# Second MLP product by Strassen's method in a phase of its own, and a mask matmul padded from 42 to 128 rows, in a two-layer trunk on one core

## Chip, cores and metric

One Trainium2 chip, one core. The metric is the device time of one execution in microseconds (us), the median of several runs.

## The reference, cut to what matters

Two layers of a diffusion trunk work on 1024 latent and 256 context tokens of width 1024, all in fp32. Each layer is a normalised input projection, four groups of heads (state-space "SSD", attention, linear recurrence, differential attention), an output projection, and an MLP with a gated residual. The context tokens are updated in layer 0 alone. What the change touches:

```python
def sq_relu_mlp(u, w1, w2):
    return jnp.square(jax.nn.relu(u @ w1)) @ w2
...
    v_l = modulate(rms_norm(h_lat, p['norm2_g']), mod_l[3], mod_l[4])
    h_lat = h_lat + mod_l[5] * sq_relu_mlp(v_l, p['w_mlp1'], p['w_mlp2'])
```

`w1` is 1024 x 4096, `w2` is 4096 x 1024.

## The kernel before

**Products.** Data lie with features on the 128 partitions and tokens along the free axis. Each fp32 operand is split into a rounded high part and the rest (`uh`, `ul`; `wh`, `wl`; `hh`, `hl`), and a product is three matmuls: high x high, high x low, low x high. The second part of a name tells the operand that lies in the array as weights, the first the one that streams.

**Order.** The class `Sched` records operations (`op`, `tt`, `stt`, `act`, `mms`, `copy`, `dma`), and `run` then writes the program: a list scheduler with planned costs (`due` gives each operation its latest start from the sum of PE costs before it) picks the operation for each engine, subject to quotas of buffers of each stream (`s.cls("S", ...)`: 30 tiles of 1288 columns; `w`, `raw`, `h`: smaller ones). An operation that may run on two engines (`copy("ANY", ...)`) goes to the one that is free first by the plan. On the chip each engine runs its own instructions in the order so fixed, and waits on semaphores. All instructions come from `_emit` (L606), so that one line stands for all of them and the profile is read by tile names. All DMAs are issued from one queue, SP.

**The MLP** (`mlp`, L1565). The normalised input `v` stands in 8 tiles (`uh`, `ul`). `m1(f)` computes 128 of the 4096 hidden features: `w_cols` loads 128 columns of `w_mlp1` (`wr`, split into `wh`, `wl`), `gemm_fm` makes 24 matmuls for each group of tokens (512, 512 and in layer 0 another 256 of context), then relu (`r`), square, and the split into `hh`, `hl`. `m2` takes two such `f`, loads two blocks of 128 rows of `w_mlp2`, and for each group of tokens and each of 8 feature tiles makes 6 matmuls in one PSUM bank, which DVE adds, times the gate `mod`, into the residual tile `hR` (self.hT), kept in SBUF. `m1` and `m2` alternate, so that nothing of the hidden layer is kept. In layer 0 the context group stands last in each `m2`. After the MLP of layer 0 comes the norm of layer 1 (squares `sq`, sums `sts`, mean `lnm`, then `lx` and `uh`, `ul`), after that of layer 1 the store: transposes `cst,hR` by PE, copies `oo`, DMAs to `out`.

**The fill** (`layer`, `fill_rate`). In layer 0 the matmuls of layer 1's modulation (`wm,cT`) are mixed into the recorded stream of operations at a rate that is set there.

**The mask matmul** (`ssd_group`). 36 times in a run a matmul of one column of `pick`, broadcast to 128 columns, with `acr`, 42 rows of cumulated decays, spreads one row over all partitions; ACT reads the bank (`wk`).

Of the kernel before, what the change touches and what calls it, by code (L numbers as in the profile page):

```python
# [10 lines left out]
F32 = mybir.dt.float32  # L11
F32R = mybir.dt.float32r
AF = mybir.ActivationFunctionType
ALU = mybir.AluOpType
# [141 lines left out]
class Sched:  # L156
# [131 lines left out]

# [1 line left out]
    def act_cost(self, out, in_, func, **kw):  # L290
# [87 lines left out]

# [1 line left out]
    def due(self):  # L380
# [226 lines left out]
NT, NL = 1280, 1024  # L607
CO, CW = 1028, 1284
GROUPS = ((0, 512), (512, 512), (1024, 256))
EPS = 1e-6  # L610
SW, WW = 1288, 1056
# [36 lines left out]
class Trunk:  # L648
# [4 lines left out]
    def __init__(self, tc, nc, A, out, pools, dbg=None):  # L653
        self.A, self.out, self.dbg = A, out, dbg or {}
        s = self.s = Sched(tc, nc)
        sb, ps = pools
        self.sb = sb
        s.cls("S", sb, 30, SW, dict(u=16, ssd=8, lru=11, sw=2, qk=4, qv=2, ssdr=1, gk=4, dk=4, gv=2, dv=1, gq=2, dq=1, mo=2, gP=4, dP=8, gT=5, dT=5, mix=16, hT=8, hid=7, x=7, wm=10, st=5))
        s.cls("w", sb, 6, WW)
        s.cls("raw", sb, 3, WW)  # L660
        s.cls("h", sb, 4, 512, dict(ln=2, lq=3, mlp=4, go=1, do=1, asq=1, ssd=3, mod=1, out=3, load=2))
        s.cls("m", sb, 8, 48, dict(ln=3, att=2, qk=4, ssd=2))
        s.psum(ps, dict(mm=(0, 1, 2, 3), m4=(0, 1, 2, 3, 4, 5), ln=(4, 5, 3), att=(3, 0), tr=(6, 7), pv=(6,), ax=(6,),
                        ssd=(4, 5), lru=(6, 7), mod=(7,), ev=(6,), qk=(3,), st=(6, 7)))
        self.nconst = 0
        self.L = [dict(), dict()]
        self.fill, self.fill_rate, self.fill_at = None, 0, 0.0
# [6 lines left out]

# [1 line left out]
    def setup(self):  # L676
        s, A = self.s, self.A
        self.cst = self.const(448, "cst")
        s.dma(self.cst.v, A["cst"])
        c = self.cst  # L680
        self.ident, self.mf, self.mb = c[:, 0:128], c[:, 128:256], c[:, 256:384]
        self.blk2, self.inv_ln, self.inv128 = c[:, 384:386], c[:, 386:387], c[:, 387:388]
        self.nhalf, self.tiny, self.ones32 = c[:, 388:404], c[:, 404:405], c[:, 406:438]
        self.pick = self.const(10, "pick", dt=F32R)[0:42, :]
        s.copy("DVE", self.pick, c[0:42, 438:448])
        self.cT = self.const(8 * 32, "cT")
        self.consts_a(0)
        x = s.tile("h", 512, F32, "load", "cx")
# [187 lines left out]

# [1 line left out]
    def split_w(self, raw, n):  # L878
# [59 lines left out]

# [1 line left out]
    def load_x(self, gi):  # L940
# [106 lines left out]

# [1 line left out]
    def conv(self, out, raw, wcols, bcol, W=CW):  # L1049
# [28 lines left out]

# [1 line left out]
    def lru_weights(self, l):  # L1080
# [73 lines left out]

# [1 line left out]
    def ssd_dt(self, l, dtraw):  # L1156
        s, L = self.s, self.L[l]
        c = self.ssdc
        dt, dta, w1, w2, w3 = (c[:, 80 * i:80 * i + 80] for i in range(5))
        nac, dec, te = w3, w2, w1  # L1160
        x = dtraw
# [4 lines left out]
        pb = s.tile("psum", 512, F32, "ssd", "pac")  # L1166
# [10 lines left out]
        R = s.tile("S", SW, F32R, "ssdr", "acr")  # L1177
        s.op("POOL", [("memset", dict(ap=R[0:42, 0:1024].f, constant=0.0))], 1300)
        n4 = nac.r("p (t d g h) -> p g d h t", t=10, d=2, g=2)
        for g in range(2):  # L1180
            pb = s.tile("psum", 512, F32, "ssd", "par")
            s.transposes([dict(out=pb[0:10, 128 * i:128 * i + 128], in_=n4[:, g, i // 2, i % 2], identity=self.ident)
                          for i in range(4)])
            hi, lo = R[0:10, 512 * g:512 * g + 512], R[32:42, 512 * g:512 * g + 512]
# [5 lines left out]
    def ssd_group(self, l, g, xs, B, C, zmake):  # L1190
        s, L = self.s, self.L[l]
# [3 lines left out]
        for src, dst, eng in ((B, Bt, "ANY"), (xs, xt, "ANY")):  # L1195
            for b0 in (0, 4, 8):
                n = min(4, 10 - b0)
# [30 lines left out]
        for i, c in enumerate(order):  # L1228
# [5 lines left out]
            pb = s.tile("psum", 512, F32, "ssd", "pbc")  # L1234
            s.mms([dict(out=pb.v, lhsT=self.pick[:, c:c + 1].bc([42, 128]), rhs=self.acr[0:42, 512 * g:512 * g + 512],
                        start=True, stop=True)])
# [58 lines left out]

# [1 line left out]
    def qk_post(self, l, bank, off, H, d, gain, t, dst, rq=None):  # L1297
# [75 lines left out]

# [1 line left out]
    def att_open(self, l, kind, idx):  # L1375
# [153 lines left out]

# [1 line left out]
    def out_proj(self, l, gis, ks):  # L1531
# [19 lines left out]
        for f in range(8):  # L1551
# [7 lines left out]
            for gi in gis:  # L1559
# [3 lines left out]
                s.stt(h, bank[:, 0:gn], self.modcol(l, 2, 0 if g0 < NL else 1, f), h, ALU.mult, ALU.add)  # L1563

    def mlp(self, l, v, gis):  # L1565
        s, A = self.s, self.A
        hid = {}

        def m1(f):
            w = self.w_cols(A["w_mlp1"][l], 128 * f)  # L1570
            hh = s.tile("S", SW, F32R, "hid", "hh")
            hl = s.tile("S", SW, F32R, "hid", "hl")
            for gi in gis:
                g0, gn = GROUPS[gi]
                bank = self.gemm_fm(w, v, g0, gn)
                r = s.tile("h", 512, F32, "mlp", "r2")
                s.relu(r[:, 0:gn], bank[:, 0:gn])
                s.tt(r[:, 0:gn], r[:, 0:gn], r[:, 0:gn], ALU.mult)
                s.copy("ANY", hh[:, g0:g0 + gn], r[:, 0:gn])
                s.tt(hl[:, g0:g0 + gn], r[:, 0:gn], hh[:, g0:g0 + gn].f, ALU.subtract)  # L1580
            hid[f] = (hh, hl)

        def m2(fs):
            ws = [self.w_rows(A["w_mlp2"][l], 128 * f) for f in fs]
            for gi in gis:
                g0, gn = GROUPS[gi]
                for ft in range(8):
                    bank = s.tile("psum", 512, F32, "m4", "pm2")
                    o = bank[:, 0:gn]
                    calls = []  # L1590
                    for f, (wh, wl) in zip(fs, ws):
                        xh, xl = hid[f][0][:, g0:g0 + gn], hid[f][1][:, g0:g0 + gn]
                        h, lo = wh[:, 128 * ft:128 * ft + 128], wl[:, 128 * ft:128 * ft + 128]
                        calls += [dict(out=o, lhsT=h, rhs=xh), dict(out=o, lhsT=h, rhs=xl), dict(out=o, lhsT=lo, rhs=xh)]
                    for i, c in enumerate(calls):
                        c.update(start=(i == 0), stop=(i == len(calls) - 1))
                    s.mms(calls)
                    h = self.hT[ft][:, g0:g0 + gn]
                    s.stt(h, o, self.modcol(l, 5, 0 if g0 < NL else 1, ft), h, ALU.mult, ALU.add)

        m1(0)
        m1(1)
        for p in range(16):
            if p < 15:
                m1(2 * p + 2)
            m2((2 * p, 2 * p + 1))
            if p < 15:
                m1(2 * p + 3)

# [18 lines left out]
    def layer(self, l):  # L1628
# [84 lines left out]
        if l == 0:  # L1713
            self.consts_a(1, self.norm_end)
            self.consts_b(1, self.norm_end)
            self.fill, self.fill_rate = itertools.chain(*[self.mod_round(1, r) for r in range(3)]), 0.5
        self.mlp(l, v, gis)
# [56 lines left out]
```

## Time and profile before

| what | us |
|---|---|
| median of 3 runs (3348.85 to 3358.43) | 3353.89 |
| span of the profiled execution (no time outside it is given) | 3352.2 |
| PE busy | 3258.6 |
| DVE busy | 2171.1 |
| ACT busy | 1166.4 |
| POOL busy | 147.1 |

A page's busy time counts an engine as busy from the start of an instruction to its modelled end, so a PE that is never idle is not a PE that could not be used better. The MLP of layer 0 runs from about 911 to 1846 us, that of layer 1 from about 2625 to 3342 us. A timeline gives the start and the duration of every instruction; the step between two starts is what a stream of them costs.

### The profile page before, as it was taken

What the parts mean: (1) busy time and instruction counts of PE and PEld (TensorE: products, weight loads), DVE (VectorE), ACT (ScalarE), POOL (GpSimd) and SP (SyncE); (2) the same over time, 40 slices, a digit from 0 to 9 for tenths busy, and PEclk for the clock granted to TensorE, in tenths of its full rate; (3) what the DMA queues carried; (4) which work ended last, traced back from release to release, by engine and by line L of the source; (5) the groups of instructions that cost most, each with busy time, mean ns of one, the idle gap of its engine ahead of it and who ended that gap; (6) DMA issues with size and microseconds to landing.
All of it is one profiled execution on the core that took longest, in us unless ns stands there. A gap on an engine that the chain in (4) does not pass through costs nothing. (4 is left out here: it accounts for less than half of the span.)

```text
span 3352.2 us, 45841 instructions
## 1 busy us (share of the span) xinstructions
PE 3258.6 (97%) x18456; PEld 2622.8 (78%) x18456; DVE 2171.1 (65%) x3785; ACT 1166.4 (35%) x2026; POOL 147.1 (4%) x168
## 2 busy tenths in 40 slices
PE   8999989999999999999999999999999999999999
PEld 6877786677688888887887888886677788888887
DVE  4787789894565555554556688689883655555554
ACT  5554447772311110101112554438771311111111
POOL 0010040000000000000000010030000000000000
PEclk9999999999999999999999989989999999999999
DMA  8443261416212222212110321151433111111111
GB/s 247 140 125 97 89 175 41 110 35 232 70 48 75 72 79 67 78 57 85 42 45 26 118 73 50 57 154 39 97 116 121 41 51 51 51 44 46 49 50 57
DMA packets 253868, 276.51 MB, mean 82 GB/s; under 512 B 22876, under 2 KB 212184, under 8 KB 253656
## 3 DMA queue, kind: packets, MB, share of 16 engines
q1 hardware_dynamic: 253656, 273.59, 27.0%
q8 instruction: 145, 2.38, 0.3%
q14 instruction: 67, 0.55, 0.1%
HBM read 218.75 MB, written 54.79 MB: 82 GB/s over the span
## 5 line engine op out<-in xcount | busy, mean ns | idle before, releaser
L606 DVE SCALAR_TENSOR_TENSOR hR<-banks,mod,hR 128x512 f32<-128x512 f32 x720 | 497.2, 697 | 420.4 <-PE banks L606 420.4
L606 PE MATMUL banks<-uh,wh 128*128 128x512 f32 (+1 forms) x1808 | 682.4, 377 | 5.8 <-ACT cvr L606 1.9
L606 PE MATMUL banks<-uh,wl 128*128 128x512 f32 (+1 forms) x1808 | 669.1, 370 | 1.7 <-DVE wl L606 1.7
L606 PE MATMUL banks<-ul,wh 128*128 128x512 f32 (+1 forms) x1808 | 669.0, 370 | 1.3 <-DVE ul L606 1.2
L606 ACT ACTIVATE wh<-wr 128x1024 fp32r<-128x1024 f32 (+2 forms) x193 | 189.5, 992 | 1050.7 <-PE banks L606 1009.9
L606 PE MATMUL banks<-hh,wh 128*128 128x512 f32 (+1 forms) x1280 | 476.7, 372 | 0.0
L606 PE MATMUL banks<-hl,wh 128*128 128x512 f32 (+1 forms) x1280 | 475.5, 371 | 0.0
L606 PE MATMUL banks<-hh,wl 128*128 128x512 f32 (+1 forms) x1280 | 474.8, 371 | 0.0
L606 PEld LDWEIGHTS banks<-uh,wh 128*128 128x128 f32 x1808 | 341.3, 189 | 98.8 <-issue 26.1
L606 PEld LDWEIGHTS banks<-uh,wl 128*128 128x128 f32 x1808 | 340.6, 188 | 65.4 <-DVE wl L606 3.0
L606 PEld LDWEIGHTS banks<-ul,wh 128*128 128x128 f32 x1808 | 341.1, 189 | 61.5 <-DVE ul L606 3.7
L606 DVE TENSOR_SCALAR_CACHE_REDUCE P<-banks,rq 128x1280 f32<-128x1280 f32 (+1 forms) x216 | 301.3, 1427 | 29.4 <-PE banks L606 28.1
L606 DVE TENSOR_TENSOR r<-r 128x512 f32<-128x512 f32 x160 | 102.2, 639 | 333.6 <-ACT r L606 331.4
L606 PEld LDWEIGHTS banks<-hh,wh 128*128 128x128 f32 x1280 | 240.8, 188 | 53.5 <-DVE hR L606 5.3
L606 ACT ACTIVATE P<-P,am 128x1280 f32<-128x1280 f32 (+1 forms) x216 | 273.4, 1272 | 21.1 <-DVE P L606 19.8
L606 PEld LDWEIGHTS banks<-hh,wl 128*128 128x128 f32 x1280 | 240.4, 188 | 44.7
L606 PEld LDWEIGHTS banks<-hl,wh 128*128 128x128 f32 x1280 | 240.6, 188 | 43.3
L606 PE MATMUL banks<-wh,uh 128*128 128x256 f32 (+2 forms) x784 | 250.4, 319 | 6.0 <-DVE qkw L606 4.2
L606 DVE TENSOR_TENSOR wl<-wr,wh 128x1024 fp32r<-128x1024 f32 (+2 forms) x204 | 230.4, 1137 | 27.6 <-ACT wh L606 26.1
L606 PE MATMUL banks<-ks,qt 128*128 128x512 f32 (+1 forms) x800 | 220.8, 387 | 20.2 <-DVE P L606 15.7
L606 PE MATMUL banks<-wl,uh 128*128 128x256 f32 (+2 forms) x784 | 226.3, 289 | 0.0
L606 PE MATMUL banks<-wh,ul 128*128 128x256 f32 (+2 forms) x784 | 225.5, 288 | 0.0
(241 smaller groups left out, 4341.0 us busy)
## 6 DMA issues: line engine op xcount, KB each, us to landing
wr<-in_w_mlp_dram SPq DMA_DIRECT2D x128, 512.0 KB
wm<-in_w_mod_dram SPq DMA_DIRECT2D x96, 512.0 KB
wr<-in_w_in_dram SPq DMA_DIRECT2D x40, 512.0 KB
ks<-dk SPq DMA_DIRECT2D x64, 160.0 KB
qt<-dq SPq DMA_DIRECT2D x72, 128.0 KB
wr<-in_w_out_dram SPq DMA_DIRECT2D x64, 128.0 KB
hd<-hT SPq DMA_DIRECT2D x8, 640.0 KB
ks<-gk SPq DMA_DIRECT2D x16, 320.0 KB
```

The costliest lines, as they stand in the source:

```text
L606: getattr(e, method)(**args)
```

## The change

The MLP becomes two phases. `mlp` first writes the residual to DRAM (`he`), which frees its 8 tiles. `mlp_up` computes, for 16 pairs of feature tiles, relu and square on 1024 tokens, takes the pair and the two halves of the tokens as a 2 x 2 block matrix, forms the sums T1 to T4 on DVE, and writes seven operands of 128 x 512 to DRAM (`hp`); the context's hidden features go there already split (`hc`). `mlp_down` then works in four quarters of four pairs. For each of seven products (A11, A12, S3, A22, S2, S1, S4; in layer 0 also A21 for the context) it forms the sum of the `w_mlp2` blocks in place (`wr`), splits it (`wa`), loads the operand (`hs`, three buffers), splits it (`kb`), makes for each of 4 column blocks 12 matmuls in a bank, and adds the bank into 14 accumulator tiles (`ka`). In the last quarter it loads the residual again (`hR`) and combines the accumulators into it. Beside this, `pick` and `acr` get 128 rows in place of 42 (the added rows of the mask are zero), and the fill rate goes from 0.5 to 0.9.

```diff
-        s.cls("S", ..., mix=16, hT=8, hid=7, x=7, wm=10, st=5))
+        s.cls("S", ..., mix=16, hT=8, hid=10, ka=14, kb=7, kr=5, kc=4, x=7, wm=10, st=5))
-        s.cls("h", sb, 4, 512, dict(ln=2, lq=3, mlp=4, go=1, ...))
+        s.cls("h", sb, 4, 512, dict(ln=2, lq=3, mlp=4, hs=3, go=1, ...))
-        self.pick = self.const(10, "pick", dt=F32R)[0:42, :]
-        s.copy("DVE", self.pick, c[0:42, 438:448])
+        self.pick = self.const(10, "pick", dt=F32R)
+        s.copy("DVE", self.pick.v, c[:, 438:448])
-        s.op("POOL", [("memset", dict(ap=R[0:42, 0:1024].f, constant=0.0))], 1300)
+        s.op("POOL", [("memset", dict(ap=R[:, 0:1024].f, constant=0.0))], 1300)
-            s.mms([dict(out=pb.v, lhsT=self.pick[:, c:c + 1].bc([42, 128]), rhs=self.acr[0:42, 512 * g:512 * g + 512],
+            s.mms([dict(out=pb.v, lhsT=self.pick[:, c:c + 1].bc([128, 128]), rhs=self.acr[:, 512 * g:512 * g + 512],
...
+    def mlp_up(self, l, v, gis):
...
+            for e in range(2):
+                w = self.w_cols(A["w_mlp1"][l], 128 * (2 * p + e))
+                r = s.tile("S", SW, F32, "hid", "hr")
...
+                    bank = self.gemm_fm(w, v, g0, gn)
+                    o = r[:, g0:g0 + gn]
+                    s.relu(o, bank[:, 0:gn])
+                    self.square(o, o)
...
+            s.tt(T1, b12, b11, ALU.subtract)
+            s.tt(T2, b22, T1, ALU.subtract)
+            s.tt(T3, b22, b12, ALU.subtract)
+            s.tt(T4, b21, T2, ALU.subtract)
+            for i, z in ((0, b11), (1, b21), (2, T3), (3, T4), (4, T2), (5, T1), (6, b22)):
+                s.dma(d[:, 512 * i:512 * i + 512], z)
...
+    def mlp_down(self, l, gis):
...
+        def halves(piece):
+            t = s.tile("w", WW, F32R, "", "wa")
+            hi, lo = t[:, 0:512], t[:, 512:1024]
+            s.copy("ANY", hi, piece)
+            s.tt(lo, piece, hi.f, ALU.subtract)
...
+        def operand(p, i):
+            h = s.tile("h", 512, F32, "hs", "hs")
+            s.dma(h.v, self.hp[p][:, 512 * i:512 * i + 512])
+            t = s.tile("S", SW, F32R, "kb", "kb")
...
+        for q in range(4):
...
+            for i, name in enumerate(("A11", "A12", "A21", "S3", "A22", "S2", "S1", "S4")):
...
+                        bank = product(ws, xs, m, 512)
+                        a = at(pi, m)
+                        if q == 0:
+                            s.copy("ANY", a, bank.v)
+                        else:
+                            s.tt(a, bank.v, a, ALU.add)
...
+                    if name == "S1":
+                        s.tt(at(5, m), at(5, m), at(4, m), ALU.add)
+                        s.tt(at(2, m), at(2, m), at(5, m), ALU.add)
+                        add(h, m + 4, 0, 512, 512, at(2, m))
+                    if name == "S4":
+                        s.tt(at(6, m), at(6, m), at(5, m), ALU.add)
+                        add(h, m, 0, 512, 512, at(6, m))
...
     def mlp(self, l, v, gis):
...
+        for k in range(8):
+            s.dma(self.hd2[k][:, 0:n], self.hT[k][:, 0:n], after=self.norm_end)
+        self.hT = None
+        self.mlp_up(l, v, gis)
+        self.flush()
+        self.mlp_down(l, gis)
...
-            self.fill, self.fill_rate = itertools.chain(*[self.mod_round(1, r) for r in range(3)]), 0.5
+            self.fill, self.fill_rate = itertools.chain(*[self.mod_round(1, r) for r in range(3)]), 0.9
```

In counts, the program has 16,410 matmul instructions where it had 16,794, and 1,337 DMA issues where it had 825.

The passage from layer 0 to layer 1 on PE, before (`hh`, `hl` with 256 columns: context part of the last `m2`; `uh`, `ul`: input projection of layer 1):

```order
L606 MATMUL banks<-hl_14026,wh_14244 128x256
L606 MATMUL banks<-hh_14024,wl_14258 128x256
L606 MATMUL banks<-hh_14301,wh_14260 128x256
L606 MATMUL banks<-hl_14303,wh_14260 128x256
L606 MATMUL banks<-hh_14301,wl_14268 128x256
L606 MATMUL banks<-uh_6411_14494,wh_14377 128x512
L606 MATMUL banks<-ul_6412_14498,wh_14377 128x512
```

The same place on PE in the changed kernel (`kb`, `wa`: last product of the latent tokens; `sq`, `sts`, `lnm`: sums, mean and broadcast of the norm):

```order
L606 MATMUL banks<-kb_15043,wa_15037 128x512 x3
L606 MATMUL banks<-sq_15137,cst_66 32x512
L606 MATMUL banks<-sq_15146,cst_66 32x512
L606 MATMUL banks<-cst_66,sts_15157 128x1 x4
L606 MATMUL banks<-cst_66,lnm_15174 128x128 x4
L606 MATMUL banks<-sq_15160,cst_66 32x512
L606 MATMUL banks<-sq_15172,cst_66 32x512
L606 MATMUL banks<-sq_15195,cst_66 32x512
L606 MATMUL banks<-sq_15202,cst_66 32x512
L606 MATMUL banks<-uh_7263_15198,wh_15050 128x512
```

The product that stood between the latent tokens' last update and the new layer is gone from there; only the norm's own small matmuls are left. On DVE the changed kernel has at this place, from the last addition of a bank (`ka<-banks`) to the first low part of the new operand (`ul`):

```order
L606 TENSOR_TENSOR ka_5991_12566<-banks,ka_5991_12566 128x512
L606 TENSOR_TENSOR ka_5991_12566<-ka_5991_12566,ka_5947_12476 128x512
L606 SCALAR_TENSOR_TENSOR hR_7026_14807<-ka_5991_12566,mod_47_142,hR_7026_14807 128x512
L606 TENSOR_TENSOR ka_5745_12036<-ka_5745_12036,ka_5937_12444 128x512
L606 TENSOR_SCALAR lnm_15174<-banks 128x4
L606 TENSOR_TENSOR ka_5745_12036<-ka_5745_12036,ka_5937_12444 128x512
L606 SCALAR_TENSOR_TENSOR hR_7027_14821<-ka_5745_12036,mod_47_142,hR_7027_14821 128x512
L606 SCALAR_TENSOR_TENSOR hR_7028_14832<-ka_5745_12036,mod_47_142,hR_7028_14832 128x512
L606 TENSOR_TENSOR ka_5750_12053<-ka_5750_12053,ka_5947_12476 128x512
L606 SCALAR_TENSOR_TENSOR lx_15190<-hR_7023_14703,gs_4643_9448,banks 128x512
L606 SCALAR_TENSOR_TENSOR lx_15193<-hR_7024_14713,gs_4643_9448,banks 128x512
L606 TENSOR_TENSOR ka_5750_12053<-ka_5750_12053,ka_5947_12476 128x512
```

Sums of accumulators, updates of the residual and the norm's `lx` share the engine here; one more update and the `ul` follow. The end of the program on DVE, before (each row takes a bank of the last `m2` into the residual):

```order
L606 SCALAR_TENSOR_TENSOR hR_9516_20568<-banks,mod_4791_10044,hR_9516_20568 128x512
L606 SCALAR_TENSOR_TENSOR hR_9517_20585<-banks,mod_4791_10044,hR_9517_20585 128x512
L606 SCALAR_TENSOR_TENSOR hR_9518_20599<-banks,mod_4791_10044,hR_9518_20599 128x512
L606 SCALAR_TENSOR_TENSOR hR_9519_20601<-banks,mod_4791_10044,hR_9519_20601 128x512
L606 SCALAR_TENSOR_TENSOR hR_9520_20606<-banks,mod_4791_10044,hR_9520_20606 128x512
```

The end on DVE in the changed kernel (`ka<-banks`: banks of the last product S4; `ka<-ka`: sums; the last 12 matmuls of PE serve all four banks):

```order
L606 TENSOR_TENSOR ka_11895_24747<-banks,ka_11895_24747 128x512 x2
L606 TENSOR_TENSOR ka_11905_24779<-banks,ka_11905_24779 128x512 x2
L606 TENSOR_TENSOR ka_11723_24370<-ka_11723_24370,ka_11851_24654 128x512 x2
L606 TENSOR_TENSOR ka_11733_24409<-ka_11733_24409,ka_11861_24688 128x512 x2
L606 TENSOR_TENSOR ka_11895_24747<-ka_11895_24747,ka_11851_24654 128x512 x2
L606 TENSOR_TENSOR ka_11905_24779<-ka_11905_24779,ka_11861_24688 128x512 x2
L606 SCALAR_TENSOR_TENSOR hR_12680_26188<-ka_11723_24370,mod_4642_9446,hR_12680_26188 128x512
L606 SCALAR_TENSOR_TENSOR hR_12681_26288<-ka_11723_24370,mod_4642_9446,hR_12681_26288 128x512
L606 SCALAR_TENSOR_TENSOR hR_12682_26297<-ka_11733_24409,mod_4642_9446,hR_12682_26297 128x512
L606 SCALAR_TENSOR_TENSOR hR_12683_26311<-ka_11733_24409,mod_4642_9446,hR_12683_26311 128x512
L606 SCALAR_TENSOR_TENSOR hR_12676_24191<-ka_11895_24747,mod_4642_9446,hR_12676_24191 128x512
```

Where one update stood behind the last bank, the additions, eight sums and eight updates stand now (the last three rows of updates are left out).

## Rows read from the trace of the kernel before

**Rows 1.** The page: busy us (share, instructions), then busy tenths in 40 slices.

```profile
PE 3258.6 (97%) x18456; PEld 2622.8 (78%) x18456; DVE 2171.1 (65%) x3785; ACT 1166.4 (35%) x2026; POOL 147.1 (4%) x168
...
DVE  4787789894565555554556688689883655555554
```

**Rows 2.** Windows: busy us (instructions) by engine, granted clock, DMA share, GB/s.

```profile
2184.00:2268.00 84.00, 74.07 (x529) 67.54 (x527) 71.50 (x182) 35.80 (x78) 30.04 (x18) 0.90 0.58 160
2772.00:2856.00 84.00, 84.00 (x364) 68.02 (x363) 45.05 (x61) 12.37 (x16) 0.00 (x0) 1.00 0.18 51
```

**Rows 3.** Waits: who waited for whom, us in total, times, longest.

```profile
ACT wh L606 <- PE banks L606: 1009.9, 131, 25.9
...
DVE hR L606 <- PE banks L606: 420.4, 581, 9.8
```

**Rows 4.** PE by form: busy us, mean ns of one.

```profile
L606 PE MATMUL banks<-hh,wh 128*128 128x512 f32 x1024 | 404.6, 395 | 0.0
...
L606 PE MATMUL banks<-hh,wl 128*128 128x512 f32 x1024 | 403.0, 394 | 0.0
```

**Rows 5.** Timeline of PE, second MLP: first and last of 19 matmuls in a row.

```profile
2899.69 0.40 PE L606 MATMUL banks<-hh,wl 128*128 128x512 f32 x1
...
2903.85 0.40 PE L606 MATMUL banks<-hh,wl 128*128 128x512 f32 x1
```

**Rows 6.** Timeline of PE between layers: first and last of 24, then layer 1.

```profile
1842.74 0.29 PE L606 MATMUL banks<-hh,wh 128*128 128x256 f32 x1
...
1845.49 0.28 PE L606 MATMUL banks<-hh,wl 128*128 128x256 f32 x1
1845.61 0.39 PE L606 MATMUL banks<-uh,wh 128*128 128x512 f32 x1
```

**Rows 7.** Mask matmul: timeline of PE, then its tile view with waiters.

```profile
405.21 0.49 PE L606 MATMUL banks<-acr,pick 42*128 42x512 f32 x1
405.63 0.38 PE L606 MATMUL banks<-wh,uh 128*128 128x256 f32 x1
...
L606 PE MATMUL banks<-acr,pick x36: 489/497/742, 263.4 to 2193.2; 42*128 42x512 f32 x36
...
  ACT wk L606: 42.1, 27
```

**Rows 8.** Timeline of the end: transposes, last update.

```profile
3341.84 1.03 PE L606 MATMUL banks<-cst,hR 128*128 128x128 f32 x8
3342.04 0.75 DVE L606 SCALAR_TENSOR_TENSOR hR<-banks,mod,hR 128x512 f32<-128x512 f32 x1 [0.64 <-PE banks L606]
```

**Rows 9.** Timeline of DVE at the second MLP's start: independent instructions in a row.

```profile
2631.76 0.69 DVE L606 TENSOR_TENSOR r<-r 128x512 f32<-128x512 f32 x1
2632.36 0.75 DVE L606 SCALAR_TENSOR_TENSOR ul<-lx,mod,uh 128x512 fp32r<-128x512 f32 x1
2633.02 1.40 DVE L606 SCALAR_TENSOR_TENSOR lx<-hR,gs,banks 128x512 f32<-128x512 f32 x2
```

**Rows 10.** Timeline of DVE, first MLP: a cast that reads the result before it.

```profile
1763.74 0.69 DVE L606 TENSOR_TENSOR r<-r 128x512 f32<-128x512 f32 x1 [2.66 <-ACT r L606]
1764.47 0.43 DVE L606 CAST hh<-r 128x512 fp32r<-128x512 f32 x1
```

**Rows 11.** Timelines of three loads: issue on SP, first user.

```profile
583.51 1.24 SPq L606 DMA_DIRECT2D qt<-gq  x2
586.12 0.60 ACT L606 ACTIVATE PT<-banks 128x512 f32<-128x512 f32 x1 [1.39 <-DMA qt<-gq]
...
627.73 0.30 SPq L606 DMA_DIRECT2D qt<-dq  x1
633.87 0.70 PE L606 MATMUL banks<-ks,qt 128*128 128x512 f32 x2 [1.75 <-DMA qt<-dq]
...
1045.50 0.42 SPq L606 DMA_DIRECT2D wr<-in_w_mlp_dram  x1
1052.52 1.06 ACT L606 ACTIVATE wh<-wr 128x1024 fp32r<-128x1024 f32 x1 [1.07 <-DMA wr<-in_w_mlp_dram]
```

More of the change, by code (lines that the diff above doesn't have):

```diff
@@ L657, in __init__ @@
         self.sb = sb
-        s.cls("S", sb, 30, SW, dict(u=16, ssd=8, lru=11, sw=2, qk=4, qv=2, ssdr=1, gk=4, dk=4, gv=2, dv=1, gq=2, dq=1, mo=2, gP=4, dP=8, gT=5, dT=5, mix=16, hT=8, hid=7, x=7, wm=10, st=5))
+        s.cls("S", sb, 30, SW, dict(u=16, ssd=8, lru=11, sw=2, qk=4, qv=2, ssdr=1, gk=4, dk=4, gv=2, dv=1, gq=2, dq=1, mo=2, gP=4, dP=8, gT=5, dT=5, mix=16, hT=8, hid=10, ka=14, kb=7, kr=5, kc=4, x=7, wm=10, st=5))
         s.cls("w", sb, 6, WW)
         s.cls("raw", sb, 3, WW)
-        s.cls("h", sb, 4, 512, dict(ln=2, lq=3, mlp=4, go=1, do=1, asq=1, ssd=3, mod=1, out=3, load=2))
+        s.cls("h", sb, 4, 512, dict(ln=2, lq=3, mlp=4, hs=3, go=1, do=1, asq=1, ssd=3, mod=1, out=3, load=2))
         s.cls("m", sb, 8, 48, dict(ln=3, att=2, qk=4, ssd=2))
@@ L1563, in out_proj @@
                 s.stt(h, bank[:, 0:gn], self.modcol(l, 2, 0 if g0 < NL else 1, f), h, ALU.mult, ALU.add)
-    def mlp(self, l, v, gis):
[L1566 to L1608, printed above, removed]
@@ new lines, in square @@
+    def square(self, out, in_):
+        s = self.s
+        o = s.act(out, in_, AF.Square)
+        kw = dict(out=out, in0=in_, in1=in_, op=ALU.mult)
+        o.alts = {"ACT": (o.calls, o.cost), "DVE": ([("tensor_tensor", kw)], s.dve_cost("tensor_tensor", **kw))}
+    def mlp_up(self, l, v, gis):
+        s, A = self.s, self.A
+        self.hp, self.hc = [], []
+        for p in range(16):
+            R = []
+            ctx = s.tile("S", SW, F32R, "hid", "hc") if 2 in gis else None
+            for e in range(2):
+                w = self.w_cols(A["w_mlp1"][l], 128 * (2 * p + e))
+                r = s.tile("S", SW, F32, "hid", "hr")
+                R.append(r)
+                for gi in gis:
+                    g0, gn = GROUPS[gi]
+                    bank = self.gemm_fm(w, v, g0, gn)
+                    o = r[:, g0:g0 + gn]
+                    s.relu(o, bank[:, 0:gn])
+                    self.square(o, o)
+                    if gi == 2:
+                        hi, lo = ctx[:, 512 * e:512 * e + 256], ctx[:, 512 * e + 256:512 * e + 512]
+                        s.copy("ANY", hi, o)
+                        s.tt(lo, o, hi.f, ALU.subtract)
+            d = s.dram(128, 7 * 512, f"hp{l}_{p}")
+            t0, t1 = slice(0, 512), slice(512, 1024)
+            b11, b12, b21, b22 = R[0][:, t0], R[0][:, t1], R[1][:, t0], R[1][:, t1]
+            x, y = s.tile("S", SW, F32, "hid", "hx"), s.tile("S", SW, F32, "hid", "hy")
+            T1, T2, T3, T4 = x[:, t0], x[:, t1], y[:, t0], y[:, t1]
+            s.tt(T1, b12, b11, ALU.subtract)
[4 more added lines that the diff above has]
+                s.dma(d[:, 512 * i:512 * i + 512], z)
+            self.hp.append(d)
+            if ctx is not None:
+                d = s.dram(128, 1024, f"hc{l}_{p}")
+                s.dma(d.v, ctx[:, 0:1024].f)
+                self.hc.append(d)
@@ L1610, in flush @@
+    def mlp(self, l, v, gis):
+        s = self.s
+        n = NT if l == 0 else NL
+        self.hd2 = [s.dram(128, NT, f"he{l}_{k}") for k in range(8)]
+        for k in range(8):
[4 more added lines that the diff above has]
+        self.mlp_down(l, gis)
     def flush(self):
```

90 lines of the change are left out of this document (added).

## The prediction

> **What bounds the kernel now.** Read the busy lines of the page first [rows 1]: TensorE (PE) is busy 97% of a span of 3352.2 us, VectorE (DVE) 65%, ScalarE (ACT) 35%. An average over stages says little, so next comes the table by stage [rows 2]. In the MLP of the second layer (the window from 2772 us) PE is busy 84.00 of 84 us at a granted clock of 1.00, DVE 45, ACT 12, and the core moves 51 GB/s. In an SSD and attention-projection stretch of the same layer PE is busy 74.07 of 84, and the clock is 0.90: at its lower level (1.2 GHz) for part of the time. Third, the waits [rows 3]: in the MLP everybody waits for PE (ACT's weight copy 1009.9 us, DVE's residual update 420.4 us). So the MLP is bound by the number of PE matmuls, and the price of one is its step, not its duration: the profile gives 395 ns for one [rows 4], but consecutive starts lie 18 steps apart in 4.16 us [rows 5], 0.231 us each. Matmuls of 256 columns step 23 times in 2.75 us, 0.120 us [rows 6], half of it, so the step is paid for columns.
>
> The profiled span is 1.7 us under the median of the runs, 3353.9; I add 1.7 at the end.
>
> **Matmuls removed.** The second product has 3 x 1024 matmuls of 512 columns now [rows 4] (the form left out there, `hl,wh`, has 1024 too). Strassen's form has 2 layers x 4 quarters x 7 products x 48 = 2688; the context product stays at 768 of 256 columns. 384 fewer at 0.231: **-88.9 us**, all on the path, since PE has no idle time there. Each carries its own weight load, which goes too. The Trainium skill (TensorE: Matmul & The Clock Gate, Back-to-back issue gap) gives a sustained 131 ns for a 512-column matmul; by it the 384 would be worth an estimated 50 us. The trace disagrees with 231 ns.
>
> **The mask matmul.** It has 42 rows of weights; the next matmul starts 0.42 us after it (405.21 to 405.63) [rows 7], at the same 512 columns that step 0.231 with 128 rows [rows 5]. If the padded one steps so too, 36 x 0.19 = 7 us of PE time go. But it stands in the SSD stretch, where ACT waits for it and PE is busy 74 of 84 [rows 2, 7]; part of it is hidden by DVE. **-3**, between 0 and -7. The Trainium skill (same page, Why this matters for your kernels) says "K=32 single mm = same time as K=128"; by that the padding would be worth nothing and the sum 3 us more. The trace shows nearly twice the step for 42 rows. The POOL memset of three times the rows is off the path (POOL 4% busy).
>
> **The end.** Before, one residual update (0.75 us) follows the last product, and the transposes run beside it [rows 8]. Now the seven products share their last 12 matmuls, and the order has on DVE after the last bank one addition, 8 sums of accumulators and 8 updates before the first transpose that needs them. An independent TENSOR_TENSOR of 512 columns steps 0.60 us though it lasts 0.69, an update 0.66 though it lasts 0.75, and one that reads the result just written 0.73 [rows 9, 10]. 0.73 + 8 x 0.60 + 8 x 0.66 = 10.8, less the 0.75 of before: **+10**, 8 to 12.
>
> **From layer 0 to layer 1.** Before, the latent tokens are finished first and the context product (24 matmuls in the rows shown) covers the norm; PE goes over with no gap [rows 6]. Now the latent product S4 is last. Behind its last matmul the order has, on DVE ahead of the first new operand, six TENSOR_TENSOR and seven updates or norm steps: 6 x 0.60 + 7 x 0.66 = 8.2 us, and within it the chain to the statistics (ACT square, PE sum, broadcast). Then each further slice of the operand costs two steps, 1.3 us, for 0.69 us of PE work (three matmuls), until a second column block is at hand. **+13**, from 8 (the DVE work alone) to 20 (with a fall of the clock to its lower level, as in [rows 2]).
>
> **DVE in the product phase.** A product of four pairs is 48 x 0.231 = 11.1 us of PE. On DVE it needs 4 low parts of weights and 4 of operands, 4 additions into accumulators (in quarter 0 copies, which ACT can take), and per quarter 16 weight sums. Quarters 0 to 2 come to at most (28 + 28 + 28 + 16) x 0.60 / 7 = 8.6 us per product, and are covered by PE. The last quarter has 28 more sums and 16 updates: 128 x 0.60 + 16 x 0.66 = 87.4, of which 10.8 stand at the end (counted above): 76.6 against 77.8 of PE. That is even; casts that the scheduler gave to DVE and dependent steps come on top. At full durations (0.69, 0.75) it is 88.1, or 10 more per layer. **+8** for both layers, 0 to 20; nearer the step, because the back-to-back rows show it.
>
> **Loads.** 512 more DMA issues on SP at about 0.4 us [rows 11] are 205 us of its queue in 1,500, no bound; nor is the bandwidth. But the operands go through three `hs` slots, and a load that waits for its slot holds up the weight loads behind it in SP's order. Counting the matmuls between the last reader of a slot and the first user of the new load, at 0.231, 28 of 224 loads have under 3.5 us of cover, in four clusters around quarter changes. A 256 KB load reached its user 2.6 us after issue, a smaller one in a busy stretch 6.1, a 512 KB one of short packets 7.0 [rows 11]. **+6**: none if 2.6 holds, 4 x (7.0 - 3.5) = 14 if 7.0 does. For the first loads of the down phase **+2** (0 to 4); the order lets the two phases overlap, so the last up-projection matmuls cover them. The spill of the residual, the operand writes and the sums T1 to T4 lie beside the up-projection, where PE has 11.1 us per half tile and DVE is under 60% busy [rows 2]; nothing. The fill rate moves weight-modulation matmuls earlier at equal count: nothing.
>
> **Sum.** -88.9 - 3 + 10 + 13 + 8 + 6 + 2 = -52.9. 3352.2 - 52.9 + 1.7 = **3301 us**.
>
> **Rivals.**
> *The new work hides.* Handoff and end at their lower bounds, DVE and loads at nothing, the mask at -7: -88.9 - 7 + 8 + 8 = -79.9, **3274**. For it: independent steps are what the order mostly has. Against: DVE is at 90% or more in only two of the page's 40 slices [rows 1], and here it would have to stay near 99% through a quarter without PE noticing.
> *DVE sets the pace.* The end, the handoff and the last quarter at their upper ends: -88.9 - 3 + 12 + 20 + 20 + 6 + 2 = -31.9, **3322**. For it: the balance above is 98% before the casts.
> *The operands arrive too late* (slower). Three slots, four loads per product: a slot may turn in 3 x 11.1 / 4 = 8.3 us. Its turn is the load's latency and the split, 0.43 + 0.60. The point from which it decides is a latency of 7.3 us. At 9 us, a product takes 4 x 10.0 / 3 = 13.4, 2.3 more than PE's, x 56 = 129 us in place of the 6: **3424**. For it: 7.0 was seen. Against: that load was double the size in short packets; 2.6 is the nearest row in size and shape.
> *A saved matmul is worth less than its step*, as that page's 131 ns would have it: 50 instead of 88.9, so **3340**. Against: the step of 256 columns is half of that of 512.
> *The change gives all of it back*: the order shows the 384 matmuls gone, so the waits would have to be 92 us instead of 39; all upper ends (20 + 12 + 20 + 14 + 4 = 70) don't reach it. About **3350**.
>
> **Chances.** The forecast 0.54, hidden work 0.20, DVE's pace 0.13, late operands 0.07, the worth of a matmul 0.02, all given back 0.04. What a measurement can tell from no change is 0.3%, 10 us. Faster: 0.54 + 0.20 + 0.13 + 0.02 = 0.89; within 0.3%: 0.04; slower: 0.07. The range runs from 3272, the hidden case, to the sum at all upper ends with no gain from the mask (-88.9 + 70 = -19, 3335); that leaves out the slower cases and a little of the others. The forecast's own range is 3286 to 3315.
>
> **What would show it.** Right: 16,410 matmul instructions in the order and, in the down phase, windows with PE over 95% busy and a 0.231 step for `kb,wa`; a DVE tail of about 11 us after the last such matmul; a gap of 8 to 20 us on PE before the first `uh` matmul of layer 1; DVE over 95% in the last quarter; the mask matmul stepping 0.23. Wrong: waits of PE for `kb` with a DMA `hs` behind them in every product (late operands); PE waiting for DVE `wa` or `ka` in quarters 0 to 2 as well; a step other than 0.231 for `kb,wa`; a granted clock under 1.00 in the down phase.

## The result: 3271.5 us, and where the time went

The changed kernel takes 3271.5 us (median of 4 runs, 3270.86 to 3274.13) against 3352.6 for the kernel before (4 runs, 3348.85 to 3358.43). The ratio is 0.9757, 95% interval 0.9745 to 0.977: 81 us faster. The forecast of 3301 had the direction and the main term right, and the time lies half a microsecond under the range.

The profiled execution has a span of 3269.5 us, 82.7 less than before. Cut at the starts of matmuls in the two PE timelines, it goes like this:

| stretch | before | after | difference |
|---|---|---|---|
| start to the first `uh` of layer 0's MLP | 898.4 | 895.5 | -2.9 |
| from there to the first `uh` of layer 1's projection | 947.2 | 909.0 | -38.2 |
| from there to the first `uh` of layer 1's MLP | 773.8 | 766.5 | -7.3 |
| from there to the end of the last product matmul's step | 722.4 | 677.5 | -44.9 |
| the end | 10.4 | 21.0 | +10.6 |

The MLPs' first `uh` matmuls stand at 898.4 and 2619.4 us in the kernel before, somewhat ahead of the 911 and 2625 that were given as their start above.

The page's busy lines and DVE's slices of the changed kernel come first, answering to [rows 1].

```profile
PE 3164.4 (97%) x18072; PEld 2552.1 (78%) x18072; DVE 2107.0 (64%) x3815; ACT 1424.0 (44%) x2540; POOL 147.9 (5%) x168
...
DVE  4697789895452222357779689689894522336888
```

PE is still busy 97%. DVE's total hardly moves, but its slices do: it is at two to three tenths over most of the stretches where the hidden features are made, and at five to nine tenths in the product phases (slices 18 to 22 and the last four). PE by form then shows what answers to [rows 4].

```profile
L606 PE MATMUL banks<-kb,wa 128*128 128x512 f32 x2688 | 652.4, 395 | 0.3 <-DVE kb L606 0.2
```

2688 matmuls of the same 395 ns, with 0.3 us of idle time ahead of them in all. Adding the steps from start to start gives 713.6 us for the 3072 `hh`, `hl` matmuls of 512 columns before and 627.4 for these: 86.2 us less, where the sum had 88.9. The Trainium skill (TensorE: Matmul & The Clock Gate, Back-to-back issue gap) would have 131 ns for each, an estimated 50 us for the 384; the trace disagrees again, at 0.233 us.

The windows of three quarters of the product phase (the last one of layer 0, the second and the last one of layer 1; columns as in [rows 2]) show what DVE did meanwhile.

```profile
1686.40:1791.50 105.10, 104.77 (x541) 85.47 (x539) 92.42 (x161) 32.88 (x54) 0.34 (x6) 1.00 0.37 118
3012.40:3090.50 78.10, 78.10 (x337) 62.95 (x336) 65.18 (x110) 26.13 (x46) 0.00 (x0) 1.00 0.46 145
3168.60:3248.50 79.90, 79.90 (x354) 64.61 (x353) 75.09 (x125) 25.34 (x44) 0.00 (x0) 1.00 0.34 108
```

In layer 1 PE does not stop in either of the two quarters shown, though DVE is 94% busy in the last one. What the order puts behind the last banks comes out behind the product. The timeline of the end, with PE's last 12 product matmuls and DVE, answers to [rows 8].

```profile
3245.61 3.04 PE L606 MATMUL banks<-kb,wa 128*128 128x512 f32 x12
...
3246.59 2.79 DVE L606 TENSOR_TENSOR ka<-banks,ka 128x512 f32<-128x512 f32 x4 [0.82 <-PE banks L606]
3249.29 4.90 DVE L606 TENSOR_TENSOR ka<-ka,ka 128x512 f32<-128x512 f32 x8
...
3254.11 5.39 DVE L606 SCALAR_TENSOR_TENSOR hR<-ka,mod,hR 128x512 f32<-128x512 f32 x8
3257.65 1.05 PE L606 MATMUL banks<-cst,hR 128*128 128x128 f32 x2 [6.73 <-DVE hR L606]
```

Eight sums in 4.9 us, eight updates in 5.4, and PE idle for 6.73 until the updates arrive: the forecast's +10, within a microsecond. DVE was not late when the last banks came: it stood idle 0.82 us before it could add the first of them. The passage from layer 0 to layer 1 on PE answers to [rows 6].

```profile
1790.74 0.96 PE L606 MATMUL banks<-kb,wa 128*128 128x512 f32 x3
1791.63 1.05 PE L606 MATMUL banks<-sq,cst 128*32 128x512 f32 x4
1793.41 1.05 PE L606 MATMUL banks<-cst,sts 128*128 128x1 f32 x8 [0.72 <-ACT sts L606]
1796.38 1.75 PE L606 MATMUL banks<-cst,lnm 128*128 128x128 f32 x8 [1.91 <-POOL lnm L606]
...
1800.69 3.83 PE L606 MATMUL banks<-sq,cst 128*32 128x512 f32 x8 [0.71 <-ACT sq L606]
1804.46 0.50 PE L606 MATMUL banks<-uh,wh 128*128 128x512 f32 x1
```

From the last product matmul (ended about 1791.5) to the first `uh` pass 13.0 us, again the forecast's number. But it is not 13 us of loss: 32 matmuls of the norm (16 of its sums, 8 of the mean, 8 broadcasts) that stood inside the MLP stage before, at 5.7 us by their steps there, stand here now. The whole stretch got 38.2 us shorter where its product matmuls alone (357.2 to 314.0 us) explain 43.2. So all the rest of it, the passage included, costs 5 us net.

What is left over is the two stretches with the SSD work: -2.9 and -7.3. The tile view of the mask matmul answers to [rows 7].

```profile
L606 PE MATMUL banks<-acr,pick x36: 388/400/502, 265.2 to 2145.5; 128*128 128x512 f32 x36
...
  ACT wk L606: 30.8, 27
```

ACT waits 11 us less for it. The padding was forecast at -3, with -7 as its bound.

### The profile page after: what moved, and what is told of

Its sections match the earlier page's. It is cut to its first block, busy times and chain, and to the rows that moved or that the text cites. A ratio compares the mean times of both kernels' runs of the same rounds, so it can differ in the third digit from the quotient of the medians.

```text
span 3269.5 us, 47003 instructions
## 1 busy us (share of the span) xinstructions
PE 3164.4 (97%) x18072; PEld 2552.1 (78%) x18072; DVE 2107.0 (64%) x3815; ACT 1424.0 (44%) x2540; POOL 147.9 (5%) x168
## 5 line engine op out<-in xcount | busy, mean ns | idle before, releaser
L606 PE MATMUL banks<-kb,wa 128*128 128x512 f32 x2688 | 652.4, 395 | 0.3 <-DVE kb L606 0.2
L606 PEld LDWEIGHTS banks<-kb,wa 128*128 128x128 f32 x2688 | 492.8, 188 | 110.9 <-issue 2.5
L606 ACT ACTIVATE wh<-wr 128x1024 fp32r<-128x1024 f32 (+2 forms) x130 | 124.7, 961 | 410.0 <-PE banks L606 260.5
L606 ACT ACTIVATE wa<-wr 128x512 fp32r<-128x512 f32 x214 | 134.3, 631 | 274.2 <-PE banks L606 231.5
L606 DVE TENSOR_SCALAR hr<-banks 128x512 f32<-128x512 f32 (+1 forms) x50 | 33.2, 665 | 307.9 <-PE banks L606 307.9
L606 PE MATMUL banks<-cst,P 128*128 128x128 f32 x1312 | 191.7, 281 | 17.8 <-ACT PT L606 10.7
L606 ACT ACTIVATE hr<-banks 128x512 f32<-128x512 f32 (+1 forms) x110 | 59.8, 543 | 325.4 <-PE banks L606 325.4
L606 PEld LDWEIGHTS banks<-cst,P 128*128 128x128 f32 x1312 | 148.5, 142 | 54.1 <-ACT PT L606 26.5
L606 DVE TENSOR_TENSOR wa<-wr,wa 128x512 fp32r<-128x512 f32 x240 | 159.9, 686 | 41.6 <-ACT wa L606 40.5
L606 PE MATMUL banks<-mx,wh 128*128 128x512 f32 (+1 forms) x640 | 185.9, 376 | 0.0
```

The source lines that it names most:

```text
L606: getattr(e, method)(**args)
```

## The experiments

Each was compared with the kernel before on the same chip; the changed kernel stands at 3271.5. A trace is of one execution. The stretch up to layer 0's MLP, which no edit from e3 on touches, takes 887.9 to 895.5 us in the traces of the change and of e3 to e11, so a few us between two traces say something only where a wait or a step is named for them.

**e1 and e2: the mask alone.** e1 is the kernel before with

```diff
-        self.pick = self.const(10, "pick", dt=F32R)[0:42, :]
+        self.pick = self.const(10, "pick", dt=F32R)
-            ... lhsT=self.pick[:, c:c + 1].bc([42, 128]), rhs=self.acr[0:42, 512 * g:512 * g + 512]
+            ... lhsT=self.pick[:, c:c + 1].bc([128, 128]), rhs=self.acr[:, 512 * g:512 * g + 512]
```

and the memset of 128 rows; e2 is the changed kernel with these lines as before.

> The kernel before with the mask matmul padded to 128 rows, nothing else. Theory (the padding shortens a chain on which ACT and DVE wait, not only PE's step): the SSD stretches of the two layers, 161 and 141 us from the first to the last mask work, get 8 and 6 us shorter as they did in the changed kernel, and the time falls by 9 to 14 us, to about 3340. Rival (the step of PE alone, partly hidden, as forecast): the time falls by 0 to 7 us, to 3346 to 3353. Second rival (the stretches moved for another reason, the new order or the clock): no change within 2 us.

> The changed kernel with the mask matmul at 42 rows again. Theory: 9 to 14 us slower than the changed kernel, about 3282. Rival (PE's step alone): 0 to 7 us slower, 3272 to 3278. Second rival (the gain in the SSD stretches is the new order's): the same as the changed kernel within 2 us.

Measured: e1 3340.5 us against 3350.8 (ratio 0.9968, 0.9956 to 0.998), 10 us faster. e2 3281.1 us, 10 us slower than the change. So the padding is worth 10 us in either kernel, and Strassen's part about 70 (e2 to before: 0.979, 0.9777 to 0.9804). Why more than the forecast's -3, and more than its bound? Timeline of PE and its weight loads (PEld) at one mask matmul in layer 1, kernel before:

```profile
2087.48 0.39 PE L606 MATMUL banks<-C,B 128*128 128x128 f32 x2
2087.79 0.18 PEld L606 LDWEIGHTS banks<-acr,pick 42*128 42x128 f32 x1
2087.80 0.50 PE L606 MATMUL banks<-acr,pick 42*128 42x512 f32 x1
...
2088.22 0.19 PEld L606 LDWEIGHTS banks<-uh,wh 128*128 128x128 f32 x1 [0.25 <-issue]
2088.22 0.50 PE L606 MATMUL banks<-uh,wh 128*128 128x512 f32 x1
...
2088.56 0.39 PE L606 MATMUL banks<-ul,wh 128*128 128x512 f32 x1
```

The same place in e1:

```profile
2082.57 0.38 PE L606 MATMUL banks<-C,B 128*128 128x128 f32 x2
2082.68 0.19 PEld L606 LDWEIGHTS banks<-acr,pick 128*128 128x128 f32 x1
2082.71 0.47 PE L606 MATMUL banks<-acr,pick 128*128 128x512 f32 x1
2082.79 0.19 PEld L606 LDWEIGHTS banks<-uh,wh 128*128 128x128 f32 x1
2083.02 0.40 PE L606 MATMUL banks<-uh,wh 128*128 128x512 f32 x1
...
2083.26 0.39 PE L606 MATMUL banks<-ul,wh 128*128 128x512 f32 x1
```

With 42 rows the weights of the mask matmul are loaded at the moment it starts (2087.79 to 2087.80), and those of the next one at the moment that one starts (2088.22): both loads stand in the open. With 128 rows the next weights are loaded at 2082.79, 0.23 us ahead of their matmul. From the pair `C,B` to the second matmul behind the mask it takes 1.08 us before and 0.69 in e1. Over all 36 places the step ahead of the mask, its own and the next one add up to 9.1 + 17.3 + 6.1 = 32.5 us before and 5.5 + 13.3 + 3.8 = 22.6 in e1: 9.9 us, the whole effect. Of these its own step gives 4.0 and its two neighbours' steps 5.9. So the size is that of the theory, but the time is PE's own, as in the rival, over three steps instead of one. Whether some other number of rows would do as well as 128, no run shows. The Trainium skill (same page, Step-by-step: what each phase is for) says that weight loads are pulled ahead of running matmuls when row groups don't conflict or the load goes to the background buffer; the lead of 0.23 us beside 0.00 agrees with there being such a condition, but no run shows which of the two the 42 rows break. The Trainium skill's other line (same page, Why this matters for your kernels), that a K of 32 takes the time of a K of 128, speaks of a single matmul; for the stream here e1 disagrees, by 9.9 us over 36 of them.

**e3: a short end.** The sums are taken before the last banks are there, and S4's banks go straight into the residual:

```diff
                     if name == "S2":
...
+                        s.tt(at(5, m), at(5, m), at(4, m), ALU.add)
                     if name == "S1":
-                        s.tt(at(5, m), at(5, m), at(4, m), ALU.add)
                         s.tt(at(2, m), at(2, m), at(5, m), ALU.add)
                         add(h, m + 4, 0, 512, 512, at(2, m))
-                    if name == "S4":
                         s.tt(at(6, m), at(6, m), at(5, m), ALU.add)
                         add(h, m, 0, 512, 512, at(6, m))
+                    if name == "S4":
+                        add(h, m, 0, 512, 512, bank.v)
```

> The changed kernel with the sums of the last quarter written so that only four updates, straight from the banks, stand behind the last product S4; the number of DVE operations is the same. Theory (the end costs what DVE has behind the last bank, 17 operations, 10 us more than before): 7 to 9 us faster than the changed kernel, about 3264, and the gap between the last product and the transposes falls from 8 us to about 2; layer 0's passage gains 0 to 2 more. Rival (DVE is the bound of the whole last quarter, so its work only shifts ahead of the end): PE waits inside the quarter instead, and the time stays within 3 us of 3271.

Measured: 3272.8 us (3268.2 to 3277.2), no gain. The timeline of its end says why:

```profile
3238.81 8.58 PE L606 MATMUL banks<-kb,wa 128*128 128x512 f32 x36
...
3247.63 2.50 DVE L606 TENSOR_TENSOR ka<-ka,ka 128x512 f32<-128x512 f32 x4
...
3250.04 2.75 DVE L606 SCALAR_TENSOR_TENSOR hR<-ka,mod,hR 128x512 f32<-128x512 f32 x4
3252.69 2.73 DVE L606 SCALAR_TENSOR_TENSOR hR<-banks,mod,hR 128x512 f32<-128x512 f32 x4
3253.59 1.04 PE L606 MATMUL banks<-cst,hR 128*128 128x128 f32 x2 [5.33 <-DVE hR L606]
```

The four updates from the banks are last, as written, but eight operations that could have been done during S4 still stand ahead of them at 3247.6, when PE is through: DVE is behind. In this profile the last quarter took 81.7 us instead of 79.9 (with eight more transposes in it), and the end 19.2 instead of 21.0. The rival holds in its time: DVE's work shifted. PE hardly waited inside the quarter for it (0.6 us).

**e4: context product last.** e3, and the context's A12 of layer 0's last quarter behind S4:

```diff
+        if cx is not None:
...
+                ws += [halves(t[:, 0:512]), halves(t[:, 512:1024])]
...
+            for m in range(4):
+                bank = product(ws, xs, m, 256)
```

> The same as e3, and in layer 0 the context's product with A12 of the last quarter (48 matmuls of 256 columns, 5.7 us of PE) is moved behind S4, with its weights and operands loaded again. Theory (the passage to layer 1 costs 6 us net because PE has nothing of its own to do in it): 2 to 5 us faster than e3, about 3260. Rival (the passage is bound by DVE, whose work the move does not shorten, and the extra splits add to it): no faster than e3, or up to 3 us slower.

In this kernel the moved product multiplies by the block A21 where A12 belongs, of the same size. Measured: 3279.8 us, 7 slower than e3. DVE, then PE, in the passage:

```profile
1791.64 2.49 DVE L606 TENSOR_TENSOR wa<-wr,wa 128x512 fp32r<-128x512 f32 x4
...
1792.38 5.54 PE L606 MATMUL banks<-kd,wa 128*128 128x256 f32 x34 [9.50 <-DVE wa L606]
```

The weights' low parts that the moved product needs were put behind the sums and updates on DVE, and PE waits 9.5 us for them. Work for PE does not help where it first needs the engine that is late.

**e5: more work for DVE** in the last quarter:

```diff
             s.tt(lo, h.v, hi.f, ALU.subtract)
+            if p >= 12:
+                s.tt(lo, h.v, hi.f, ALU.subtract)
```

> The changed kernel, with the low part of each operand of the last quarter computed twice: 28 more DVE operations of 0.60 us in each layer, 17 us, in a quarter where DVE was busy 75.1 of 79.9 us (layer 1) and 92.5 of 105.1 (layer 0). Theory after e3 (DVE, not PE, sets when the last quarter is over, and its backlog comes out behind the last product): layer 1 gets 12 us longer, layer 0 5 to 12, so 3288 to 3296. Rival (PE's step sets the pace, DVE's work shifts into earlier quarters where it has 15 to 30% of room): no more than 5 us slower.

Measured: 3303.8 us (3299.9 to 3309.2), 32 us slower for 34 us of added DVE work, more than the theory's 17 to 24. The windows of the two last quarters, layer 0 and layer 1:

```profile
1683.10:1793.60 110.50, 105.56 (x537) 86.77 (x536) 102.62 (x173) 33.65 (x58) 0.00 (x0) 0.98 0.36 113
3188.00:3281.10 93.10, 84.81 (x353) 66.57 (x352) 89.70 (x147) 26.18 (x46) 0.00 (x0) 0.96 0.31 94
```

In layer 1 the quarter grows by 13.2 us (79.9 to 93.1) and the end stays at 21 us. In layer 0 the quarter grows by 5.4 and the passage from 13.0 to 25.9. So with 17 us more, DVE sets when a last quarter and what follows it are over. In the change layer 1 had about 4 us of room (17 less 13.2; the window above leaves 79.9 - 75.1 = 4.8), and layer 0's quarter and passage together had none (5.4 + 12.9 = 18.3 for 17).

**e6, e7, e9, e10: less work for DVE.** The operands of the last quarter are split in the up phase and stored as high and low parts (e6 with e3's end, e7 with the end of the change; e9 as e6 in layer 1 alone; e10 as e9 and, in layer 0, for two of its four pairs):

```diff
+                if split:
+                    t = s.tile("S", SW, F32R, "hid", "hz")
+                    hi, lo = t[:, 0:512], t[:, 512:1024]
+                    s.copy("ANY", hi, z)
+                    s.tt(lo, z, hi.f, ALU.subtract)
+                    s.dma(d[:, 1024 * i:1024 * i + 1024], t[:, 0:1024].f)
...
+            if p >= 12:
+                t = s.tile("S", SW, F32R, "kb", "kb")
+                s.dma(t[:, 0:1024].f, self.hp[p][:, 1024 * i:1024 * i + 1024])
+                return t[:, 0:512], t[:, 512:1024]
```

> e3 (four updates behind the last product) with, in addition, the 28 operands of the last quarter split into high and low parts in the up phase, where DVE is half idle, and loaded as they are: 28 subtractions (17 us) and 28 casts less in the last quarter of each layer, 256 KB more per load. Theory (DVE's backlog of the last quarter is what made e3 gain nothing): now the end shrinks to about 3 us behind the last product, and the time is 3258 to 3263, 8 to 13 us under the changed kernel. Rival (the end is bound by something else, or the longer loads cost what DVE gains): 3268 to 3275.

> The changed kernel with the last quarter's operands split in the up phase, and the sums of the results written as in the change. Theory: DVE comes to the end without a backlog of its own, but the sums and updates that the order puts behind the last bank stay there: 2 to 6 us faster than 3271. Rival (the backlog alone was the end): as fast as e6. Second rival (the larger loads hurt): slower than 3271.

Measured: e6 3265.9 us (3263.6 to 3275.1), e7 3272.3 (3269.3 to 3276.6). By the traces the layers went opposite ways. In e6 the end is 10.7 us, as before the change, instead of 21.0; in layer 0 the last quarter and the passage take 125.7 us instead of 118.1. Windows of e6's last quarters, and the longest idle time of PE in layer 0's:

```profile
1686.10:1803.10 117.00, 110.41 (x561) 89.88 (x559) 82.28 (x141) 24.68 (x40) 2.49 (x8) 0.96 0.49 168
3180.60:3262.60 82.00, 80.77 (x362) 65.43 (x361) 68.16 (x108) 17.92 (x30) 0.00 (x0) 1.00 0.56 198
```

```profile
1762.52 17.62 PE L606 MATMUL banks<-kb,wa 128*128 128x512 f32 x63 [5.76 <-DMA kb<-hp]
```

DVE falls from 75 to 68 us busy in layer 1, and the backlog is gone. In layer 0 PE waits 5.8 us for a load of a split operand, the late operand that the forecast had as a rival. The loads are of double size, and four of them leave SP's queue only behind the eight loads of the residual:

```profile
1735.35 17.48 SPq L606 DMA_DIRECT2D hR<-he  x8
1752.92 2.89 SPq L606 DMA_DIRECT2D kb<-hp  x4
```

The trace of e6 is of a run of 3275.1 us, 9 over its median. But e7's trace, of a run near its median, has the same wait:

```profile
1755.83 18.67 PE L606 MATMUL banks<-kb,wa 128*128 128x512 f32 x72 [4.82 <-DMA kb<-hp]
```

In e7 the end shrinks by 5 us, because the planned order has only four sums and four updates behind the last banks there, and layer 0 loses 5, so that nothing is left. Neither the order of e3 alone (end 19.2 us) nor the split operands alone (15.8) bring the end back to 10.7: it takes both.

> e6 with the pre-split operands in layer 1 alone, layer 0 loads and splits as in the change. Theory (in e6 layer 1 gained 8 us and layer 0 lost 8, the latter to a PE wait of 5.8 us for a 512 KB load in its last quarter, where the context's tiles leave fewer buffers): 3262 to 3265, faster than the change by 7 to 10 us in every run. Rival (e6's loss in layer 0 came from the new order of the sums, not from the loads): 3268 to 3272.

> e9, and in layer 0 half of the last quarter's operands pre-split (14 subtractions, 8.5 us of DVE, less there). Theory (DVE sets when layer 0's last quarter and its passage are over, if loads keep up): 2 to 6 us faster than e9. Rival (the longer loads wait for buffers as in e6): as e9, or up to 5 us slower.

Measured: e9 3263.9 us (3260.1 to 3266.6), ratio 0.9732 (0.9716 to 0.9747), the fastest of all kernels here, 7.6 us under the change by the medians (4.9 to 11.4 in single runs, so not the 7 to 10 in every run); the two intervals just touch. e10 3267.8 (ratio 0.9741, 0.9725 to 0.9758) and e6 (0.9751, 0.9731 to 0.9772) are not to be told from e9 by their times. That e6's loss in layer 0 comes from the loads and not from the order of the sums is shown by traces alone: e3, with the order and without the loads, takes 118.0 us there, and e7, with the loads and without the order, 122.8, against 118.1 in the change. The end of e9 on PE:

```profile
3245.14 2.35 PE L606 MATMUL banks<-kb,wa 128*128 128x512 f32 x9
3247.33 1.03 PE L606 MATMUL banks<-cst,hR 128*128 128x128 f32 x8
3248.61 1.15 PE L606 MATMUL banks<-cst,hR 128*128 128x128 f32 x8 [0.25 <-ACT oo L606]
```

No gap: the transposes follow as in [rows 8], and 11.0 us after the last product the program ends.

**e8: two slots for loads**, the quota `hs=3` set to 2.

> The changed kernel with two buffers for loaded operands in place of three. A slot may now turn in 2 x 11.1 / 4 = 5.5 us. Theory (a load needs 2.7 to 3.5 us when the queue is free, and the split 1.0, so the third slot is reserve): within 4 us of 3271. Rival (the loads are near their limit, as the late-operand case of the prediction has it, with 7 us now and then): 15 us slower or more, with PE waiting for the operands in the middle of the quarters.

Measured: 3270.7 us (3269.4 to 3276.2): no effect beyond the spread of the runs, so the third slot is reserve. In its trace layer 0's last quarter and passage take 122.5 us instead of 118.1, but the longest waits of PE there are for ACT's squares `sq`, not for loads. In the change three loads issued in a row at 1754 us, behind the residual's, reached their first user 7.3 us later, and ACT had waited for them; timeline of SP and ACT:

```profile
1736.57 16.01 SPq L606 DMA_DIRECT2D hR<-he  x7
1754.22 1.52 SPq L606 DMA_DIRECT2D hs<-hp  x3
...
1761.51 2.08 ACT L606 ACTIVATE kb<-hs 128x512 fp32r<-128x512 f32 x3 [0.94 <-DMA hs<-hp]
```

PE had its operands in hand all the same. A latency as feared occurs in two of the seven places where a user waited for such a load (7.3 and 6.9 us; 2.7 to 4.0 in the others), and the operands already split in the seven `kb` buffers behind the slots cover it.

**e11: the fill rate** back at 0.5 in the changed kernel.

> The changed kernel with the fill rate at 0.5 as before. Theory (the same modulation matmuls at another place in a phase where PE is always busy, at equal count): 3271, within 3 us. Rival (at 0.5 a rest of them falls behind the up phase and delays the first products): 3 to 10 us slower.

Measured: 3282.8 us (3277.6 to 3287.0), 11 slower. By the trace the first quarter of layer 0's product phase takes 108.3 us instead of 101.9, its modulation matmuls end at 1379 instead of 1302, and PE waits:

```profile
1388.83 4.08 PE L606 MATMUL banks<-kb,wa 128*128 128x512 f32 x9 [4.09 <-ACT wa L606]
```

That is 6 of the 11; the rest is spread over later stretches, and its cause was not looked for further.

## Why the forecast was wrong, step by step

The main mechanism was right and the sum was 30 us too high: the added costs were taken too dear and the mask's gain too small.

- **Matmuls removed, -88.9.** Right: -86.2 by steps (384 x 0.231 is 88.7, so the sum was 0.2 off by itself); the new matmuls step 0.233 us where the old ones stepped 0.232.
- **The end, +10.** Right: +10.6, by the rows named, with DVE done 11 us behind the last product as forecast.
- **The passage, +13.** The gap was 13.0 us, the cost 5. The step that failed: the whole gap was counted as loss, though the changed order printed ahead of the forecast shows the norm's own matmuls in it, 5.7 us that had been paid for elsewhere before.
- **DVE in the last quarter, +8.** It cost nothing: PE idles 0.33 us in layer 0's last quarter and not at all in layer 1's. The balance itself, 76.6 us of DVE work against 77.8, was near the truth (75.1 busy of 79.9 in layer 1). What failed is the surcharge for casts and dependent steps on top of it, which was set between 0 and 20 without a row of its own. The signs had DVE over 95% busy; it was 94% in layer 1 and 88% in layer 0. It was also luck by a few us: by e5 there were about 4 us of room in layer 1, and none in layer 0's quarter and passage together.
- **Loads, +6, and the first products, +2.** Nothing that PE's waits show. The cover was computed for the slots alone, without the split operands that wait in `kb`; e8 took a slot away and the time stayed. That SP's order holds loads up was right (e6, e8), but behind the residual's loads, not at the quarter changes. The first products are covered because of the new fill rate, which the forecast held for neutral: e11 shows 6 us at that place, 11 in all.
- **The mask, -3, bound -7.** -10, as e1 and e2 show. The bound took the matmul's own step, and at 0.23 us; that step became 0.28 (median) and gave 4.0 us. Its neighbours' steps, 5.9 of the 9.9 us, stood in the timeline from which [rows 7] is taken and were not read. This is what put the result under the range: with -10 in place of -7, its lower end would have been 3269.

Passage 8, DVE 8, loads and start 8, mask 7, less 3 for the matmuls, make 28 of the 30 us. The other 2 lie in layer 1's MLP (-44.9, of which its product matmuls explain 42.9), and no row was found for them. The rival "the new work hides", 3274, was the nearest; e5 shows that it hid at the very edge.

## What to carry to other kernels

When an engine is loaded to the limit just before a serial end, draw up one balance for the stage and the end together: work that is moved ahead of the last product finds no room there (e3). Add work to that engine to see how much room it has (e5), and move work off it into an idle phase to gain room (e9). When a gap appears between stages, subtract the work that moved into it. A matmul with few rows is paid by its neighbours too: read three steps, not one.

## What was not expected of the hardware

A matmul with 42 rows of weights keeps the weight loads on both sides of it from running ahead: the lead of a load over its matmul falls from 0.11 us (its own, median of 36) and 0.23 us (the next one's) to 0.00. Beside that, 150 more MB moved (277 to 430 in the page's totals) and 512 more DMA issues cost no PE time that the trace shows.
